# A two-block transformer on one core: ten planning rounds, weight chunks split ahead of the norms, and a shared scaling

## The chip, the cores and the metric

The kernel runs on one core of one Trainium2 chip. The metric is the device time of one execution in microseconds; of several runs the median is taken. Engines are called as in the profile: PE is TensorE (PEld its weight loads), DVE is VectorE, ACT is ScalarE, POOL is GpSimd, and SP is SyncE, whose queue issues most transfers (SPq).

## What is computed

One sequence of 512 tokens with 1024 channels passes two blocks, all in float32. The first block has two layers; each is a mixing part and a feed-forward part (FFN):

```python
h = rms_norm(x, norm_mix[l]) * (1.0 + sc1) + sh1
proj = h @ w_in[l]                      # delta-rule heads, windowed attention, gates
...
x = x + gt1 * (merged @ w_o[l])
h = rms_norm(x, norm_ffn[l]) * (1.0 + sc2) + sh2
up_act, up_lin = jnp.split(h @ w_up[l], 2, axis=-1)
up_act = causal_dwconv(up_act, ffn_conv[l]) + ffn_conv_b[l]
x = x + gt2 * ((jax.nn.silu(up_act) * up_lin) @ w_down[l])
```

The mixing part runs a gated delta rule over 8 heads in chunks and a sliding-window attention with sinks. The second block is one layer of the same make: norm, `w_in_2`, a banded attention, a state-space branch, gates, `w_out_2`, final norm. Scales and shifts (sc, sh, gt) come from `w_ada`.

## The kernel before

**Arithmetic.** A float32 product is made of three passes at a faster matmul type: weights and activations are split into a high part (`whi`, `hhi`) and a rest (`wlo`, `hlo`), and hi x hi, hi x lo and lo x hi are added up in PSUM. `chunk` (line 546) loads a weight chunk of 128x1024 elements into a `raw` tile from SP's queue, and `split` (line 539) makes `whi` by a copy on ACT and `wlo` by a subtraction on VectorE. `raw`, `whi` and `wlo` have three buffers each.

**GEMMs.** `gemm_f` (line 564) gives feature-major output, 256 columns of weights at a time: eight row tiles in two chunks of four, two PSUM tiles `gf`. With `split` it does the first 256 tokens of all chunks, then the other 256. `gemm_t` (line 600) gives token-major output in four PSUM tiles `gt`, one for each 128 tokens; the last `last` chunks are held, and each token tile is finished and passed on in turn.

**Seams.** `residual` (line 1421) calls `add` (line 1396): two `gemm_t` over the two halves of 512 output columns, with gate and addition into the x tiles on VectorE and the sum of squares on ACT. In the second half `done` calls `norm` (line 752) for the tile before: add and power on VectorE and POOL (`nsum`), scaling into `xn` on VectorE, four transposes `ntr` on TensorE for each half of the channels, scale and shift (VectorE for the first half, ACT for the second), `hhi` on ACT, `hlo` on VectorE. The next stage's matmuls need this h. There are four such seams: after mixing and after the FFN, in each layer. The next stage is `ffn` with `w_up`, then `delta_front` with columns 1024 on of `w_in`, and after the last FFN `second` with columns 2048 on of `w_in_2`; each begins with `gemm_f(..., split=True)`.

**Order.** Nothing is issued directly. A `Recorder` keeps all operations with their dependencies and a modelled duration (`cost`, line 112); `plan` (line 202) is a list scheduler that goes through time, takes on each engine the ready operation with the smallest priority `prio`, models buffers, transfers and ACT's function tables, and gives one order of all; `emit` (line 353) issues it. The priority is the place in the program, and tiles of one tag get their buffers in program order. All instructions come from line 359, so the profile's groups are told apart by tile names. `step` (line 633), called by every `chunk`, moves background work (the products with `w_ada`, tables of the state space) forward.

**The first norm** is another routine (`first_norm`, line 759); it leaves chunks of two row tiles in `self.pre`, from which `gemm_f` takes them in place of loading.

Of the kernel before, what the change touches and what calls it, by code (L numbers as in the profile page):

```python
# [50 lines left out]
LAT = {"PE": 54.0, "DVE": 35.0, "ACT": 60.0, "POOL": 110.0, "SP": 60.0}  # L51
SLACK = {"PE": 0.0, "DVE": 0.0, "ACT": 0.0, "POOL": 0.0, "SP": 0.0}
TABLES = {"Exp": ("exp",), "Tanh": ("exp", "silu", "gelu"), "Silu": ("silu",), "Sin": ("silu", "trig"), "Gelu_apprx_tanh": ("gelu",)}
# [3 lines left out]
class Op:  # L57
    __slots__ = ("n", "eng", "name", "call", "dur", "over", "lock", "dep", "succ", "left", "ready", "tiles", "need", "prio", "start", "mode", "bytes", "team", "lead", "wait", "tables")

# [19 lines left out]
class Recorder:  # L79
# [121 lines left out]

    def plan(self):
        import heapq
        ops = self.ops
        for o in ops:
            o.left = len(o.dep)
            o.ready = 0.0
            for p in o.dep.values():
                p.succ.append(o)

        uses, order, bufs, place = {}, {}, {}, {}
        for o in ops:
            o.need = []
            for t in o.tiles:
                nm = t.name
                if nm not in uses:
                    uses[nm] = 0
                    tag = t.tag
                    order.setdefault(tag, []).append(nm)
                    bufs[tag] = t.bufs or t.tag_meta.bufs  # L220
                    place[nm] = tag, len(order[tag]) - 1
                uses[nm] += 1
                o.need.append(place[nm])

        pend = None
        for o in ops:
            o.lead, o.team = o, [o]
            if o.eng != PE_E:
                continue
            key = o.tiles[-1].name, o.mode  # L230
            if pend and pend[1] == key and all(p.n < pend[0].n or p.eng == PE_E for p in o.dep.values()):
                o.lead = pend[0]
                o.lead.team.append(o)
            else:
                pend = (o, key) if o.mode != (128, 128) else None
        for o in ops:
            o.left -= sum(p.lead is o.lead for p in o.dep.values())
            o.lead.wait = len(o.lead.team)
        freed = {g: [0.0] * b for g, b in bufs.items()}
        turn = {g: 0 for g in bufs}  # L240
# [8 lines left out]
        mode, table = (128, 128), "exp"  # L249
        count = 0  # L250

        def offer(o):

            while o.need:
# [8 lines left out]
                since[tag, k] = t = heapq.heappop(freed[tag])  # L263
                turn[tag] += 1
                o.ready = max(o.ready, t)
                o.need.pop()
# [19 lines left out]
        seq = []  # L286
        import collections
        while count < len(ops):
# [11 lines left out]
            if best is None:  # L300
                raise RuntimeError("no plan: slots %s" % {g: (turn[g], len(order[g]), sorted(parked.get(g, {}))[:3]) for g in turn if parked.get(g)})
            s, e = best
# [4 lines left out]
            if e in held:  # L307
                other = held[POOL_E if e == DVE_E else DVE_E]
                if other > s + 140 and ops[av[0][1]].lock:
                    free = [x for x in av if not ops[x[1]].lock]  # L310
                    if free:
                        x = min(free)
                        av.remove(x)
                        heapq.heapify(av)
                        heapq.heappush(av, (-1, x[1]))
            p, n = heapq.heappop(av)
            for o in ops[n].team:
                o.start = s = max(s, clock[e])
                d = o.dur
                if e == PE_E and o.mode != mode:  # L320
# [5 lines left out]
                if o.lock:  # L326
                    s = max(s, held[POOL_E if e == DVE_E else DVE_E] - 140)
                    held[e] = s + d
                end = s + d
                clock[e] = end - o.over  # L330
                if o.name == "dma_start":
                    dma_free = max(dma_free, end) + o.bytes / 340.0
                    end = max(dma_free, end) + (2300 if e == SP_E else 2600)
                count += 1
                seq.append(o)
                for t in o.tiles:
# [3 lines left out]
                    if not uses[nm]:  # L340
                        heapq.heappush(freed[t.tag], last_end[nm])
                        wake(t.tag)
                for q in o.succ:
                    if q.lead is o.lead:
                        continue
                    q.left -= 1
                    q.ready = max(q.ready, clock[e] if q.eng == e == PE_E else end + LAT[q.eng] + (0 if q.eng == e else SLACK[q.eng]))
                    if not q.left:
                        offer(q)
        self.end = max(clock.values())  # L350
        return seq

# [18 lines left out]
class Net:  # L371
# [166 lines left out]

    def split(self, raw, n, eng=None):
        hi = self.p_hi.tile([128, 1024], F32R, name="whi", tag="whi")  # L540
        lo = self.p_lo.tile([128, 1024], F32R, name="wlo", tag="wlo")
# [4 lines left out]
    def chunk(self, parts, kk, n, eng=None):  # L546

# [7 lines left out]
        hi, lo = self.split(raw, kk * n, eng)  # L555
        self.step()
        return self.views(hi, lo, kk, n)

    @staticmethod
# [4 lines left out]
    def gemm_f(self, w, c0, act, consume, ntile=2, parts=None, split=False):  # L564
# [3 lines left out]
        for g in range(ntile // 2):  # L568
            ps = [self.Gp("gf") for _ in range(2)]
            c = c0 + g * 256  # L570
            cols = [(c, 256)] if parts is None else [(p, 128) for p in parts]
            m = 2 if (w.tensor.name, c, 0) in self.pre else 4
            groups = [(k0, min(m, kt - k0)) for k0 in range(0, kt, m)]

            def load(k0, n):
                if (w.tensor.name, c, k0) in self.pre:
                    return self.pre.pop((w.tensor.name, c, k0))
                return self.chunk([w[k0 * 128:(k0 + n) * 128, p:p + m] for p, m in cols], n, 256)
# [173 lines left out]
    def norm(self, xt, t, ss, a, b, h):  # L752
        rs = self.norm_scale(ss)
        for q in range(2):
            xn = self.t2("xn")
            self.tsc(xn, xt[:, q * 512:q * 512 + 512], rs, MUL)
            self.norm_half(xn, t, q, a, b, h)

    def first_norm(self, x0):
# [47 lines left out]
        for q in range(4):  # L807
# [10 lines left out]
            for c in (1024, 0):  # L818
                self.pre[w.tensor.name, c, 2 * q] = self.chunk([w[q * 256:q * 256 + 256, c:c + 256]], 2, 256, self.G)
            apply(q, row)  # L820
# [485 lines left out]
    def mixing(self, l, xin, xout, hact):  # L1306
# [88 lines left out]

    def add(self, w, act, xs, g=None, done=None):

        ss = [self.ts("nss", 2) for _ in range(4)]
        for c in range(2):
            o = slice(c * 512, c * 512 + 512)  # L1400

            def f(t, ps):
# [7 lines left out]
                if done:  # L1410
# [10 lines left out]
    def residual(self, w, act, xs, xout, g, a, b):  # L1421

# [5 lines left out]

        self.add(w, act, xs, g, done)
        return h  # L1430

    def ffn(self, l, hact, xin, xout):
# [551 lines left out]
```

## Time and profile before

| | us |
|---|---|
| median of three runs | 2430.78 |
| lowest and highest | 2430.03, 2432.83 |
| the profiled execution | 2433.17 |
| its span, first to last instruction | 2431.4 |

| engine | busy us | instructions |
|---|---|---|
| TensorE | 2364.1 | 13388 |
| VectorE | 1644.6 | 3087 |
| ACT | 1012.2 | 2095 |
| POOL | 522.9 | 719 |

Busy time counts the union of an engine's instructions. Matmuls overlap one another, so a busy TensorE may still be slowed; the granted clock (PEclk, a share of 2.4 GHz) tells one such slowing. In a timeline row the bracket gives the idle time of the engine ahead of the instruction and what ended it.

### The profile page before, as it was taken

What the parts mean: (1) busy time and instruction counts of PE and PEld (TensorE: products, weight loads), DVE (VectorE), ACT (ScalarE), POOL (GpSimd) and SP (SyncE); (2) the same over time, 40 slices, a digit from 0 to 9 for tenths busy, and PEclk for the clock granted to TensorE, in tenths of its full rate; (3) what the DMA queues carried; (4) which work ended last, traced back from release to release, by engine and by line L of the source; (5) the groups of instructions that cost most, each with busy time, mean ns of one, the idle gap of its engine ahead of it and who ended that gap; (6) DMA issues with size and microseconds to landing.
All of it is one profiled execution on the core that took longest, in us unless ns stands there. A gap on an engine that the chain in (4) does not pass through costs nothing.

```text
span 2431.4 us, 35819 instructions
## 1 busy us (share of the span) xinstructions
PE 2364.1 (97%) x13388; PEld 1928.4 (79%) x13388; DVE 1644.6 (68%) x3087; ACT 1012.2 (42%) x2095; POOL 522.9 (22%) x719
## 2 busy tenths in 40 slices
PE   7999999999999999999999999999999998999998
PEld 4878777778888887887888787888888888877786
DVE  3898899676666577468888955566555546765454
ACT  5544454533443233354446454334323323264432
POOL 1322424204100000213232421050051613500000
PEclk9999999999999999999999999999999999999999
DMA  7322225456446556332222333445334344532242
GB/s 251 99 66 77 84 71 161 139 168 200 156 153 197 180 181 187 118 103 74 66 75 79 89 111 96 130 170 184 114 109 127 117 146 146 173 113 79 78 139 78
DMA packets 239742, 309.10 MB, mean 127 GB/s; under 512 B 32144, under 2 KB 189712, under 8 KB 239568
## 3 DMA queue, kind: packets, MB, share of 16 engines
q1 hardware_dynamic: 228864, 275.64, 37.0%
q0 software_dynamic: 10416, 30.91, 3.5%
q8 instruction: 106, 1.74, 0.3%
q14 instruction: 68, 0.56, 0.1%
q10 hardware_dynamic: 288, 0.26, 0.0%
HBM read 276.20 MB, written 30.56 MB: 126 GB/s over the span
## 4 chain that ended last, share of the span: by engine, by line
PE 84%; DVE 7%; DMA 3%; ACT 2%; issue 2%; SPq 1%; POOL 1%; DVEq 0%; POOLq 0%; ACTq 0%
PE gf L359 54%; PE gt L359 18%; PE sc L359 1%; SPq L359 1%; PE pvo L359 1%; PE ada L359 1%; DMA pn<-nd 1%; PE zps L359 1%; PE osps L359 1%; PE kqs L359 1%; PE yps L359 1%; DVE wlo L359 1%; PE qktr L359 1%; PE gram L359 1%; DVE ua L359 1%
## 5 line engine op out<-in xcount | busy, mean ns | idle before, releaser
L359 PE MATMUL gf<-hhi,whi 128*128 128x512 f32 (+1 forms) x1888 | 720.8, 384 | 11.8 <-ACT whi L359 8.5
L359 PE MATMUL gf<-hlo,whi 128*128 128x512 f32 (+1 forms) x1888 | 720.6, 382 | 0.2 <-DVE hlo L359 0.2
L359 PE MATMUL gf<-hhi,wlo 128*128 128x512 f32 (+1 forms) x1888 | 719.9, 382 | 0.1
L359 DVE TENSOR_TENSOR wlo<-raw,whi 128x1024 fp32r<-128x1024 f32 (+1 forms) x358 | 461.8, 1291 | 339.2 <-ACT whi L359 336.1
L359 ACT ACTIVATE whi<-raw 128x1024 fp32r<-128x1024 f32 (+1 forms) x366 | 378.6, 1036 | 655.7 <-PE gf L359 310.5
L359 PEld LDWEIGHTS gf<-hhi,whi 128*128 128x128 f32 x1888 | 358.3, 191 | 76.2 <-ACT whi L359 10.0
L359 PEld LDWEIGHTS gf<-hlo,whi 128*128 128x128 f32 x1888 | 359.1, 190 | 60.7 <-issue 2.1
L359 PEld LDWEIGHTS gf<-hhi,wlo 128*128 128x128 f32 x1888 | 359.0, 190 | 59.4 <-DVE wlo L359 0.6
L359 PE MATMUL gt<-whi,g 128*128 128x512 f32 x704 | 220.1, 392 | 0.0
L359 PEld LDWEIGHTS gt<-whi,g 128*128 128x128 f32 x704 | 132.2, 188 | 27.2
L359 PE MATMUL gt<-wlo,g 128*128 128x512 f32 x352 | 137.4, 390 | 0.0
L359 DVE SCALAR_TENSOR_TENSOR acc<-raw,csil,acc 128x1024 f32<-128x1024 f32 x70 | 90.7, 1295 | 34.8 <-DMA raw<-in_w_ada_dram 34.6
L359 DVE SCALAR_TENSOR_TENSOR cacc<-gf,vec,cacc 128x511 f32<-128x511 f32 x144 | 106.8, 743 | 7.9 <-ACT cacc L359 6.6
L359 PE MATMUL gt<-whi,hhi 128*128 128x512 f32 (+1 forms) x288 | 107.1, 374 | 1.0 <-DVE gx L359 1.0
L359 PE MATMUL gt<-wlo,hhi 128*128 128x512 f32 (+1 forms) x288 | 107.6, 374 | 0.0
L359 PE MATMUL gt<-whi,hlo 128*128 128x512 f32 (+1 forms) x288 | 107.5, 375 | 0.0
L359 PE MATMUL gf<-rhi,whi 128*128 128x512 f32 x256 | 99.9, 390 | 0.0
L359 PE MATMUL gf<-rhi,wlo 128*128 128x512 f32 x256 | 99.8, 390 | 0.0
L359 PE MATMUL gf<-rlo,whi 128*128 128x512 f32 x256 | 99.8, 390 | 0.0
L359 DVE SCALAR_TENSOR_TENSOR facc<-gf,vec,facc 128x511 f32<-128x511 f32 x88 | 65.7, 748 | 37.2 <-ACT facc L359 35.6
L359 PEld LDWEIGHTS gt<-wlo,g 128*128 128x128 f32 x352 | 66.2, 188 | 13.5 <-issue 0.2
L359 POOL DMA_DIRECT2D acc<-in_b_ada_dram x4 | 2.1, 525 | 288.3 <-DVE wlo L359 283.5
(414 smaller groups left out, 3802.4 us busy)
## 6 DMA issues: line engine op xcount, KB each, us to landing
raw<-in_w_in_dram SPq DMA_DIRECT2D x140, 512.0 KB, 3.7
raw<-in_w_ada_dram SPq DMA_DIRECT2D x80, 512.0 KB, 4.0
raw<-in_w_up_dram SPq DMA_DIRECT2D x80, 512.0 KB, 4.2
raw<-in_w_down_dram SPq DMA_DIRECT2D x40, 512.0 KB, 3.7
wa<-in_w_ada_dram SPq DMA_DIRECT2D x32, 256.0 KB, 6.0
raw<-in_w_dn_out_dram SPq DMA_DIRECT2D x16, 512.0 KB, 3.5
raw<-in_w_swa_out_dram SPq DMA_DIRECT2D x16, 512.0 KB, 4.8
raw<-in_w_o_dram SPq DMA_DIRECT2D x16, 512.0 KB, 3.8
```

What stands on the lines that cost most here:

```text
L359: i = f(*a, **k).ins
```

## The change

Three things, in one diff.

- The planner runs up to ten rounds (`ROUNDS`). Each operation off TensorE is taken 30 ns longer (`MARGIN`), and a hand-over from one engine to another 30 ns longer (`SLACK`). After a round, `late` goes backward through the order and gives each operation a latest start, from its successors, the next operation on its engine and the next user of its buffers; the new priority is the mean of the old one (in the first round the start) and this. Buffers of a tag are then handed out in the order of the last plan. The plan with the earliest modelled end is issued; a round that finds no plan ends the loop.
- `ahead` loads and splits the first 256 columns of the next stage's weights (two chunks of four row tiles) just before the second `gemm_t` of `residual`, into tiles of their own: one buffer of each b4 lane and one of tag `ua`. `gemm_f` finds them in `self.pre` (the key now holds the offset of the layer, too).
- In `norm` the scaled tile `xn` of the second half is made by ACT (`Copy` with a scale), no longer by VectorE.

```diff
+MARGIN, SLACK = 30.0, 30.0
+ROUNDS = 10
...
             for o in ops[n].team:
-                o.start = s = max(s, clock[e])
-                d = o.dur
+                s = max(s, clock[e])
+                d = o.dur + (0 if e == PE_E else MARGIN)
...
+    def late(self, seq):
+
+        late, after = {}, {}
+        for o in reversed(seq):
+            took, x = o.end - o.start, self.end
+            f = after.get(o.eng)
+            if f is not None:
+                x = late[f.n] - min(f.start - o.start, o.dur - o.over)
+            for q in o.succ:
+                if q.eng != o.eng or q.eng != PE_E:
+                    x = min(x, late[q.n] - took - LAT[q.eng])
+            for t in o.tiles:
+                if t.name in self.then:
+                    x = min(x, late[self.first[self.then[t.name]]] - took - 60)
+            late[o.n] = x
+            after[o.eng] = o
+        return late
+
+    def plan(self):
+
+        self.prepare()
+        tags, best = self.tags, None
+        for k in range(ROUNDS):
+            seq = self.schedule(tags)
+            if seq is None:
+                break
+            if best is None or self.end < best[0]:
+                best = self.end, seq
+            self.first, tags = {}, {}
+            for o in seq:
+                for t in o.tiles:
+                    if t.name not in self.first:
+                        self.first[t.name] = o.n
+                        tags.setdefault(t.tag, []).append(t.name)
+            late = self.late(seq)
+            for o in self.ops:
+                o.prio = 0.5 * ((o.prio if k else o.start) + late[o.n])
+        self.end, seq = best
         return seq
...
+    def ahead(self, w, c):
+
+        pair = self.p_qk.tile([128, 2, 1024], F32R, name="wah", tag="ua", bufs=2)
+        homes = ((self.b4("wah", (128, 1024), F32R, "f"), self.b4("wah", (128, 1024), F32R, "x")), (pair[:, 0], pair[:, 1]))
+        for i, home in enumerate(homes):
+            self.pre[w.tensor.name, w.offset + c, 4 * i] = self.chunk([w[i * 512:i * 512 + 512, c:c + 256]], 4, 256, home=home)
...
             xn = self.t2("xn")
-            self.tsc(xn, xt[:, q * 512:q * 512 + 512], rs, MUL)
+            if q:
+                self.act(xn, xt[:, 512:1024], AF.Copy, scale=rs)
+            else:
+                self.tsc(xn, xt[:, 0:512], rs, MUL)
...
-        return self.residual(io["w_o"][l], mh, self.load_x(xin, "x"), xout, g, *self.mods(l, 1))
+        return self.residual(io["w_o"][l], mh, self.load_x(xin, "x"), xout, g, *self.mods(l, 1), (io["w_up"][l], 0))
...
+            if c and nxt:
+                self.ahead(*nxt)
             self.gemm_t([w[:, o]], act, f, last=2 + c)
...
-        h = self.residual(wd[c:FF], g, xs, xout, gr, a, b)
+        nxt = (io["w_in"][l + 1], 1024) if l + 1 < DEPTH else (io["w_in_2"][0], 2048)
+        h = self.residual(wd[c:FF], g, xs, xout, gr, a, b, nxt)
```

## Rows read from the trace of the kernel before

**Rows 1.** The page's first part: busy us, share of span, instructions.
```profile
span 2431.4 us, 35819 instructions
PE 2364.1 (97%) x13388; PEld 1928.4 (79%) x13388; DVE 1644.6 (68%) x3087; ACT 1012.2 (42%) x2095; POOL 522.9 (22%) x719
```

**Rows 2.** Window view: length, busy us by engine, PEclk, DMA share, GB/s.
```profile
0.00:48.00 48.00, 35.03 (x181) 19.16 (x182) 12.05 (x35) 28.17 (x50) 9.42 (x16) 1.00 0.91 292
48.00:640.00 592.00, 580.22 (x3709) 467.75 (x3708) 474.48 (x1053) 269.49 (x686) 174.03 (x209) 1.00 0.39 118
640.00:660.00 20.00, 15.61 (x83) 13.53 (x82) 17.28 (x35) 12.68 (x27) 3.62 (x5) 0.83 0.70 241
652.00:658.00 6.00, 4.84 (x22) 4.55 (x23) 5.39 (x10) 2.20 (x6) 0.27 (x1) 0.50 0.81 250
...
1015.00:1050.00 35.00, 28.91 (x162) 24.90 (x161) 22.81 (x48) 17.39 (x37) 6.34 (x8) 0.90 0.36 115
1050.00:1638.00 588.00, 583.24 (x3782) 473.41 (x3781) 435.38 (x990) 265.11 (x675) 161.89 (x192) 1.00 0.33 98
1638.00:1660.00 22.00, 17.64 (x116) 16.33 (x116) 15.27 (x31) 11.75 (x26) 3.17 (x4) 0.84 0.63 216
1660.00:2003.00 343.00, 343.00 (x1619) 285.01 (x1618) 188.82 (x217) 119.86 (x156) 93.74 (x205) 1.00 0.41 129
2003.00:2038.00 35.00, 29.05 (x154) 25.45 (x153) 22.21 (x48) 14.91 (x36) 7.33 (x8) 0.85 0.37 126
2038.00:2290.00 252.00, 246.75 (x1360) 199.88 (x1360) 162.10 (x272) 111.35 (x196) 47.89 (x44) 1.00 0.38 119
```

**Rows 3.** Timeline of the first seam: start us, duration us, instruction, idle before.
```profile
646.65 0.39 PE L359 MATMUL gt<-whi,mlo 128*128 128x512 f32 x1
...
650.63 2.35 DVE L359 TENSOR_TENSOR wlo<-raw,whi 128x1024 fp32r<-128x1024 f32 x2
...
651.87 0.55 PE L359 MATMUL gf<-hhi,whi 128*128 128x256 f32 x1 [3.23 <-ACT whi L359]
...
658.85 1.29 DVE L359 TENSOR_TENSOR hlo<-xn,hhi 128x512 fp32r<-128x512 f32 x2 [1.45 <-ACT hhi L359]
```

**Rows 4.** Timeline of the fourth seam, TensorE's two waits.
```profile
2020.51 1.09 PE L359 MATMUL gf<-hhi,whi 128*128 128x256 f32 x4 [2.24 <-ACT hhi L359]
...
2028.54 1.94 PE L359 MATMUL ntr<-cst,xn 128*128 128x128 f32 x8 [3.07 <-DVE xn L359]
```

**Rows 5.** Groups by form: count, busy us, mean ns, idle before.
```profile
L359 DVE TENSOR_TENSOR wlo<-raw,whi 128x1024 fp32r<-128x1024 f32 x344 | 450.8, 1312 | 314.8 <-ACT whi L359 311.9 <-PE bt L359 1.6
...
L359 DVE TENSOR_SCALAR xn<-x,nsum 128x512 f32<-128x512 f32 x32 | 14.7, 482 | 5.3 <-POOL nsum L359 5.3
...
L359 ACT ACTIVATE whi<-raw 128x1024 fp32r<-128x1024 f32 x344 | 363.8, 1059 | 619.1 <-PE gf L359 309.1 <-PE gt L359 184.0 <-issue 53.8
...
L359 ACT ACTIVATE cacc<-gf,vec 128x512 f32<-128x512 f32 x48 | 32.9, 685 | 22.5 <-PE gf L359 20.2 <-DVE vt L359 1.5 <-POOL kd L359 0.3
```

**Rows 6.** Timeline, third seam: two neighbours of the 256-column matmuls.
```profile
1654.09 0.28 PE L359 MATMUL gf<-hhi,whi 128*128 128x256 f32 x1
1654.21 0.28 PE L359 MATMUL gf<-hlo,whi 128*128 128x256 f32 x1
```

**Rows 7.** Timeline of the first mixing stage: a wait and a long operation.
```profile
105.75 2.12 DVE L359 TENSOR_SCALAR pn<-pn 64x256 f32<-64x256 f32 x1 [2.88 <-DMA pn<-nd]
...
110.78 0.66 PE L359 MATMUL qktr<-cst,qk 128*128 128x128 f32 x4 [2.35 <-DVE xi L359]
```

More of the change, by code (lines that the diff above doesn't have):

```diff
@@ L57 @@
 class Op:
-    __slots__ = ("n", "eng", "name", "call", "dur", "over", "lock", "dep", "succ", "left", "ready", "tiles", "need", "prio", "start", "mode", "bytes", "team", "lead", "wait", "tables")
+    __slots__ = ("n", "eng", "name", "call", "dur", "over", "lock", "dep", "succ", "left", "ready", "tiles", "need", "prio", "start", "end", "mode", "bytes", "team", "lead", "wait", "tables")
 class Eng:
@@ L199, in add, with prepare @@
         return o
-    def plan(self):
-        import heapq
+    def prepare(self):
         ops = self.ops
         for o in ops:
-            o.left = len(o.dep)
-            o.ready = 0.0
             for p in o.dep.values():
                 p.succ.append(o)
-        uses, order, bufs, place = {}, {}, {}, {}
+        self.uses, self.bufs, self.tags = {}, {}, {}
         for o in ops:
-            o.need = []
             for t in o.tiles:
                 nm = t.name
[L216 to L223, printed above, removed]
+                if nm not in self.uses:
+                    self.uses[nm] = 0
+                    self.tags.setdefault(t.tag, []).append(nm)
+                    self.bufs[t.tag] = t.bufs or t.tag_meta.bufs
+                self.uses[nm] += 1
         pend = None
@@ L235, in plan, with schedule @@
                 pend = (o, key) if o.mode != (128, 128) else None
+    def schedule(self, tags):
+        import heapq
+        ops, bufs = self.ops, self.bufs
+        uses = dict(self.uses)
+        place = {nm: (g, k) for g, names in tags.items() for k, nm in enumerate(names)}
         for o in ops:
-            o.left -= sum(p.lead is o.lead for p in o.dep.values())
+            o.need = [place[t.name] for t in o.tiles]
+            o.ready = 0.0
+            o.left = len(o.dep) - sum(p.lead is o.lead for p in o.dep.values())
             o.lead.wait = len(o.lead.team)
-        freed = {g: [0.0] * b for g, b in bufs.items()}
+        freed = {g: [(0.0, "")] * n for g, n in bufs.items()}
         turn = {g: 0 for g in bufs}
@@ L250, in plan @@
         count = 0
+        self.then = {}
         def offer(o):
@@ L262, in offer @@
                     return
-                since[tag, k] = t = heapq.heappop(freed[tag])
+                since[tag, k], old = heapq.heappop(freed[tag])
+                self.then[old] = tags[tag][k]
                 turn[tag] += 1
-                o.ready = max(o.ready, t)
+                o.ready = max(o.ready, since[tag, k])
                 o.need.pop()
@@ L300, in plan @@
             if best is None:
-                raise RuntimeError("no plan: slots %s" % {g: (turn[g], len(order[g]), sorted(parked.get(g, {}))[:3]) for g in turn if parked.get(g)})
+                return None
             s, e = best
@@ L328, in plan @@
                     held[e] = s + d
+                o.start = s
                 end = s + d
@@ L333, in plan @@
                     end = max(dma_free, end) + (2300 if e == SP_E else 2600)
+                o.end = end
                 count += 1
@@ L346, in plan @@
                     q.left -= 1
-                    q.ready = max(q.ready, clock[e] if q.eng == e == PE_E else end + LAT[q.eng] + (0 if q.eng == e else SLACK[q.eng]))
+                    q.ready = max(q.ready, clock[e] if q.eng == e == PE_E else end + LAT[q.eng] + (0 if q.eng == e else SLACK))
                     if not q.left:
@@ L536, in rsqrt, with split @@
         return m
-    def split(self, raw, n, eng=None):
-        hi = self.p_hi.tile([128, 1024], F32R, name="whi", tag="whi")
-        lo = self.p_lo.tile([128, 1024], F32R, name="wlo", tag="wlo")
+    def split(self, raw, n, eng=None, home=None):
+        hi, lo = home or (self.p_hi.tile([128, 1024], F32R, name="whi", tag="whi"),
+                          self.p_lo.tile([128, 1024], F32R, name="wlo", tag="wlo"))
         self.act(hi[:, :n], raw[:, :n], AF.Copy)
@@ L554, in chunk @@
             o += c
-        hi, lo = self.split(raw, kk * n, eng)
+        hi, lo = self.split(raw, kk * n, eng, home)
         self.step()
         return self.views(hi, lo, kk, n)
+    def ahead(self, w, c):
[3 more added lines that the diff above has]
+            self.pre[w.tensor.name, w.offset + c, 4 * i] = self.chunk([w[i * 512:i * 512 + 512, c:c + 256]], 4, 256, home=home)
     @staticmethod
@@ L1419, in add, with residual @@
             done(3, ss[3])
-    def residual(self, w, act, xs, xout, g, a, b):
+    def residual(self, w, act, xs, xout, g, a, b, nxt):
         h = self.new_h()
@@ L1427, in done @@
             self.norm(xs[t], t, ss, a, b, h)
-        self.add(w, act, xs, g, done)
+        self.add(w, act, xs, g, done, nxt)
         return h
```

20 lines of the change are left out of this document (10 added, 10 removed).

## The prediction

> **What bounds the kernel now.** I read the page's busy table first: TensorE is busy 2364.1 of 2431.4 us [rows 1], so at most 67 us are idle, and the other engines matter only where TensorE waits for them. Next I cut the span into stages with the window view [rows 2]. In the pure matmul stage from 1660 to 2003 TensorE is busy 343.00 of 343.00 us, while VectorE has 188.82 and ACT 119.86: nothing there can be gained by ordering, and both helpers have room. The loss stands at the four seams, where a norm turns x into the next h and every further matmul needs that h: 640 to 660 (after mixing, layer 0), 1015 to 1050 (after the FFN, layer 0), 1638 to 1660 and 2003 to 2038 (the same in layer 1).
>
> A seam costs twice: idle time, and after it matmuls at a lower clock. From 652 to 658 the granted clock is 0.50, the 1.2 GHz level, right behind a 3.23 us wait [rows 2, 3]. So I price a seam as (window minus PE busy) plus (1 minus PEclk) times window. First: 4.39 + 0.17 x 20 = 7.8. Second: 6.09 + 0.10 x 35 = 9.6. Third: 4.36 + 0.16 x 22 = 7.9. Fourth: 5.95 + 0.15 x 35 = 11.2. Sum 36.5 us. Outside, the two mixing stages idle 11.8 and 4.8 us and the second block 5.3 [rows 2], together 21.9.
>
> What ends the waits: at the first seam TensorE has done a few matmuls of the next stage when it stops for whi, from ACT, until 651.87 [rows 3]. The weights had to be split in the seam itself, between norm operations, because all three whi buffers hold the last w_o chunks to the end; wlo is written at 650.63, in the middle of the norm. At the fourth seam it waits 2.24 us for hhi of an early tile, then 3.07 us at the transposes of the last tile, behind xn [rows 4].
>
> **Part 1, two chunks ahead.** ahead() loads and splits the first column group of the next GEMM (two chunks, 4 x 128 rows by 256 columns each) before the chunks of the second half of the residual GEMM, into homes of its own. It issues two loads on SP's queue, two ACT copies of 1.06 us and two VectorE subtractions of 1.31 us [rows 5]; they are only moved, no byte is added. In the plan's first order they stand ahead of the residual GEMM's own loads on SP: those wait behind them if a raw buffer is late. Cover: the matmul stages, with VectorE busy 55% and ACT 35% [rows 2]; without it a seam would pay 2 x (1.06 + 1.31) = 4.7 us, as now. On the seam the 3.23 us wait at 651.87 goes, and I take the third seam for its twin (idle 4.36 against 4.39 [rows 2]). What is late next is h of the last tile. Built from rows, its chain after the last residual matmul is two VectorE passes of some 0.69, ACT's square about 0.8, the sum and power about 0.8, the scale 0.7, transposes 0.6, four scalings 1.4, hhi 0.6 and hlo 0.7: about 7 us, with a dozen hand-overs about 8.5 (an estimate; the 0.65 us of one hlo is half the 1.29 of [rows 3], the other pieces are close to such passes). Measured today it is longer: at the first seam the last hlo begins at 658.85, 12 us after the last residual matmul at 646.65 [rows 3], since ACT and VectorE do four splits in between. Against it TensorE has the first token half of two column groups, 2 x 48 matmuls at 0.12 us [rows 6] = 11.5 us. The second of these groups still needs whi and wlo in the seam, but has 5.7 us for it and finds the three whi buffers free and its loads done. So I let nearly all go, but not the wait for the early tile, which no weight cures: I leave 1.5 us at each mixing seam and 3.0 at each FFN seam (the 2.24 plus a hand-over), 9.0 in all. Gain 36.5 - 9.0 = 27.5 us. Bounds: 12 if only the first group is covered (rival B), 36.5 if no loss is left.
>
> **Part 2, the shared scale.** For the second half of each row tile xn moves from VectorE to ACT: 16 instructions of 0.482 us [rows 5] leave VectorE, and ACT gets 16. The trace has no ACT copy of this shape with a per-row scale from SBUF; nearest is the 128x512 one with a scale at 0.685 us [rows 5]. One tile's two halves then take 0.69 side by side instead of 2 x 0.482 in a row: 0.3 us off a tile's chain. Behind it on ACT wait the scalings and hhi of the same tile; if it queues behind a 1.06 us split, the chain loses up to 0.8 instead. I take nothing (bounds from 1 us less to 3 us more over the four seams, since one tile a seam is exposed).
> The row says VectorE is the fuller engine in the seam, 17.28 of 20 us against ACT's 12.68 [rows 2]. The Trainium skill (Perfetto Trace Analysis, Optimizing Scalar/DVE Operations) says that an operation for which VectorE has a fast mode is quicker there, and that moving it to ACT pays if VectorE is saturated. By its first half the move loses 0.2 us each on ACT, by its second it gains; at 86% I read the row as near the second, and neither changes the sum.
>
> **Part 3, ten plans.** The order on every engine is fixed at build time by a list scheduler. Its priority was the place in the program; now it becomes, in nine further rounds, the mean of the old priority and a latest start computed backward from the end, buffers may be handed out in the order of the last plan, each non-TensorE operation gets 30 ns margin, and each hand-over between engines 30 ns. Kept is the plan that ends first by the planner's own clock. No instruction is added or removed. What can it win on the chip? Only the 21.9 us idle outside the seams, and waits where the planner was wrong: at 110.78 TensorE waits 2.35 us for a transpose's input, because VectorE was held by a 2.12 us operation on 64x256 [rows 7], far over the 0.482 of the 128x512 one [rows 5]. A margin of 30 ns doesn't cover such an operation, but small lateness it does. Bounds: all 21.9 gone, or the same again added. Nearest to the truth I think is a fifth gone: 4 us. At the head (idle 13 of 48 us, DMA share 0.91 [rows 2]) the transfers decide, so I take 0, within 3 either way.
>
> **The sum.** The profiled execution took 2433.2 us (span 2431.4 and 1.8 around it): 2433.2 - 27.5 - 4 = 2401.7. The median of the runs is 2430.8, 2.4 lower, so 2399.
>
> **Rivals.**
> A, the forecast: 2399. Chance 0.42.
> B, only the first group is covered. ACT and VectorE come to the second group's split too late, as they did at 650.63 [rows 3]; TensorE then has 5.7 us against a chain of about 10, idles 4 us per seam and pays some 2 more at the low clock: 24 of 36.5 us stay. 2430.8 - 12 - 4 = 2415. For it: VectorE's 86%; against: four splits become two. Chance 0.20.
> C, the new orders also clear two thirds of the idle time outside: 2430.8 - 27.5 - 15 = 2388. For it: with program order a chain step goes as soon as it is ready, so each lateness becomes a wait; with latest starts some stand further back. Chance 0.16.
> D, it does not do what it says: the homes of the early chunks come free only at the seam (they take the last buffer of three tags) and the new plans shift waits about. 2431, give or take 5. Against: x, its row and the activations leave one buffer each. Chance 0.10.
> E, slower. Rounds chosen by a clock that takes 0.29 us (152 + 0.53 x 256 ns, in cost) for an operation that took 2.12 put more matmuls behind late VectorE results in the mixing stages. A wait like that of rows 7 costs 2.35 us, and half of a low-clock stretch behind it; at the first seam that stretch was 2 x 0.17 x 20 = 6.8 us, and I take one half as long, so 1.7 us. At 4 us each, 8 new ones eat the 31.5 us gain; 12 give 2430.8 + 48 - 31.5 = 2447. Chance 0.12. The Trainium skill (TensorE: Matmul & The Clock Gate, Architectural detail) says that matmuls keep their order and that VectorE and ACT work strictly first in, first out, which is what makes one misplaced instruction hold all behind it; the 2.35 us row agrees.
>
> **How the numbers follow.** 0.2% (4.9 us) is about what measurements of this kernel can tell from no change. A, B and C lie below 2425.9, and a little of D: faster 0.79. Same 0.09, most of D. Slower 0.12, E. The range leaves out E and the far end of C: 2376 to 2432.
>
> **What would show it.** Right: no TensorE wait for whi at the seams, PEclk near 1.00 in windows of 20 to 35 us there, PE idle in them under 3 us each, the same matmul count, ACT with 16 more xn. Part 3 shows in idle time of the two mixing stages, 16.6 us now. Wrong: a half-clock stretch left at three or four seams (B, D), or mixing stages that are longer with new waits over 1 us (E).

## The result, and the profile after

The changed kernel takes 2453.31 us (2449.80 to 2455.23), the kernel before beside it 2430.41 us: ratio 1.0089, 95% interval 1.0074 to 1.0104. It is slower by 0.89%, some 22 us, where the forecast said faster by 32. The profiled execution took 2451.6 us, and this is its first part (us, share of the span, instructions):

```profile
span 2449.8 us, 35838 instructions
PE 2369.8 (97%) x13388; PEld 1947.0 (79%) x13388; DVE 1637.8 (67%) x3071; ACT 1020.1 (42%) x2111; POOL 517.7 (21%) x719
```

Against [rows 1] the work is the same: as many matmuls, sixteen instructions moved from VectorE to ACT. So the 18.4 us of the two spans are waiting and low clock. The window view of the changed kernel, with windows laid about the same work as in [rows 2] (length, busy us by engine, granted clock, DMA share, GB/s); the eighth is a part of the first:

```profile
48.00:652.00 604.00, 587.75 (x3702) 480.55 (x3701) 464.68 (x1052) 270.56 (x684) 168.01 (x197) 0.97 0.39 117
652.00:673.00 21.00, 16.86 (x95) 14.62 (x94) 16.62 (x34) 15.50 (x33) 4.94 (x5) 0.84 0.64 216
1027.00:1062.00 35.00, 29.11 (x181) 25.88 (x180) 20.82 (x43) 19.91 (x42) 6.66 (x9) 0.95 0.35 108
1062.00:1650.00 588.00, 578.11 (x3751) 475.54 (x3750) 438.86 (x985) 264.62 (x677) 163.79 (x190) 0.99 0.33 98
1650.00:1672.00 22.00, 17.66 (x109) 15.81 (x108) 15.72 (x32) 13.16 (x28) 4.37 (x4) 0.84 0.60 195
1672.00:2027.00 355.00, 347.14 (x1632) 288.25 (x1631) 194.71 (x218) 119.29 (x155) 89.07 (x204) 0.99 0.41 127
2027.00:2062.00 35.00, 30.30 (x172) 26.34 (x171) 20.70 (x44) 17.76 (x40) 4.82 (x12) 0.90 0.39 130
410.00:455.00 45.00, 35.16 (x332) 27.53 (x332) 25.06 (x60) 14.40 (x33) 7.39 (x16) 0.63 0.27 80
```

PEclk has two decimals, too coarse for 600 us, so I summed for each stage what a matmul takes to the next one's start beyond the median of its kind (its output tile) and shape; I call that the excess. It holds idle time and low clock together. The stages are the windows of [rows 2] and of the view above; the second block is 2062 to 2314 in the changed kernel.

| stage | excess before, us | after |
|---|---|---|
| first mixing stage | 38.8 | 52.8 |
| second mixing stage | 29.7 | 34.2 |
| the four seams | 7.8, 10.2, 7.1, 10.9 = 36.0 | 7.1, 8.4, 7.5, 8.5 = 31.5 |
| second FFN's matmul stage | 1.0 | 11.6 |
| second block | 12.6 | 10.4 |
| all of the program | 139.1 | 160.4 |

The seams, where 27.5 us were to come from, gave 4.5. Two places lost more than that, and the second mixing stage lost as much.

**The end of the first mixing stage.** From 410 to 455 us TensorE is busy 35.16 of 45 us at a clock of 0.63; in the kernel before the like stretch reads:

```profile
400.00:445.00 45.00, 41.84 (x241) 33.16 (x240) 33.79 (x98) 24.67 (x55) 18.26 (x33) 0.99 0.47 145
```

The timeline of the changed kernel there (start, duration, instruction, idle before):

```profile
444.58 2.07 PE L406 MATMUL kqs<-st,qk 128*128 128x128 f32 x8 [0.44 <-DVE st L406]
...
451.42 2.07 PE L406 MATMUL kqs<-st,qk 128*128 128x128 f32 x8 [0.44 <-DVE st L406]
453.10 1.09 ACT L406 ACTIVATE mb<-gf 128x512 f32<-128x512 f32 x2 [1.88 <-PE kqs L406]
...
453.75 0.79 PE L406 MATMUL gf<-hhi,whi 128*128 128x512 f32 x1 [0.26 <-ACT mb L406]
```

These are the steps of the delta recurrence, one behind the other, and no gf matmul of the gates between them. Each lasts 6.8 us, with TensorE at the 1.2 GHz level:

```profile
430.00:453.00 23.00, 19.22 (x91) 16.70 (x92) 5.32 (x17) 5.78 (x14) 0.58 (x1) 0.50 0.09 28
```

The next gate GEMM comes only when ACT empties its PSUM tile into mb, and ACT's wait before that is put down by the profile to the recurrence's last kqs.

**The second FFN.** TensorE waits 7.86 us for one wlo (same view):

```profile
1844.24 0.69 DVE L406 TENSOR_TENSOR xm<-gt,grow 128x512 f32<-128x512 f32 x1 [1.10 <-PE gt L406]
1844.97 9.15 DVE L406 TENSOR_TENSOR x<-x,xm 128x512 f32<-128x512 f32 x1
1845.05 0.31 POOL L406 TENSOR_TENSOR sbb<-sbb,stmp 128x64 f32<-128x64 f32 x1
...
1856.38 0.79 PE L406 MATMUL gf<-hhi,wlo 128*128 128x512 f32 x1 [7.86 <-DVE wlo L406]
```

The addition x + xm, mostly 0.69 us, takes 9.15, beside a run of 30 POOL operations of the state-space tables. VectorE's next wlo is late by that much.

**The first seam.** The whi wait of [rows 3] is gone, as forecast, and others stand there:

```profile
663.38 2.67 POOL L406 TENSOR_TENSOR nsum<-nsum,mhalf 128x1 f32<-128x1 f32 x1 [0.57 <-DVE nsum L406]
664.48 0.80 PE L406 MATMUL gf<-hhi,wlo 128*128 128x256 f32 x2 [2.27 <-DVE wlo L406]
...
666.86 1.97 PE L406 MATMUL ntr<-cst,xn 128*128 128x128 f32 x8 [1.58 <-ACT xn L406]
```

### The profile page after: what moved, and what is told of

The parts are those of the page before. It is cut to its first block, busy times and chain, and to the rows that moved or that the text cites. A ratio compares the mean times of both kernels' runs of the same rounds, so it can differ in the third digit from the quotient of the medians.

```text
span 2449.8 us, 35838 instructions
## 1 busy us (share of the span) xinstructions
PE 2369.8 (97%) x13388; PEld 1947.0 (79%) x13388; DVE 1637.8 (67%) x3071; ACT 1020.1 (42%) x2111; POOL 517.7 (21%) x719
## 4 chain that ended last, share of the span: by engine, by line
PE 90%; DVE 3%; ACT 2%; DMA 2%; issue 2%; SPq 0%; POOL 0%; DVEq 0%; POOLq 0%; ACTq 0%
PE gf L406 57%; PE gt L406 19%; PE sc L406 1%; PE osps L406 1%; PE gram L406 1%; PE pvo L406 1%; PE kqs L406 1%; PE zps L406 1%; PE yps L406 1%; PE xps L406 1%; PE ada L406 1%; PE ntr L406 1%; PE bs L406 1%; DMA wa<-in_w_ada_dram 1%; PE qktr L406 1%
## 5 line engine op out<-in xcount | busy, mean ns | idle before, releaser
L406 PE MATMUL gf<-hhi,wlo 128*128 128x512 f32 (+1 forms) x1760 | 682.3, 389 | 13.8 <-DVE wlo L406 13.8
L406 PE MATMUL gf<-hlo,whi 128*128 128x512 f32 (+1 forms) x1760 | 682.9, 389 | 0.3 <-DVE hlo L406 0.3
L406 PE MATMUL gf<-hhi,whi 128*128 128x512 f32 (+1 forms) x1760 | 682.1, 390 | 1.1 <-ACT mb L406 0.7
L406 DVE TENSOR_TENSOR wlo<-raw,whi 128x1024 fp32r<-128x1024 f32 (+2 forms) x350 | 444.6, 1270 | 318.9 <-ACT whi L406 317.8
L406 ACT ACTIVATE whi<-raw 128x1024 fp32r<-128x1024 f32 (+2 forms) x358 | 370.6, 1037 | 625.8 <-PE gf L406 360.7
L406 PEld LDWEIGHTS gf<-hhi,wlo 128*128 128x128 f32 x1760 | 333.2, 189 | 75.2 <-DVE wlo L406 15.3
L406 PEld LDWEIGHTS gf<-hlo,whi 128*128 128x128 f32 x1760 | 332.7, 189 | 64.0 <-issue 3.6
L406 PEld LDWEIGHTS gf<-hhi,whi 128*128 128x128 f32 x1760 | 333.0, 190 | 62.8 <-ACT hhi L406 2.3
L406 DVE SCALAR_TENSOR_TENSOR cacc<-gf,vec,cacc 128x511 f32<-128x511 f32 (+1 forms) x144 | 106.1, 742 | 18.1 <-ACT cacc L406 17.0
L406 DVE SCALAR_TENSOR_TENSOR acc<-raw,csil,acc 128x1024 f32<-128x1024 f32 x70 | 91.8, 1311 | 31.6 <-DMA raw<-in_w_ada_dram 31.0
L406 ACT ACTIVATE pp<-sc,snm 128x128 f32<-128x128 f32 x128 | 45.5, 365 | 46.5 <-DVE snm L406 36.5
```

The source lines that it names most:

```text
L406: i = f(*a, **k).ins
```

## The experiments

All times are medians; the ratio is to the kernel before on the same chip. "One round" is ROUNDS = 1, that is, priority by place in the program as in the kernel before; "no margins" is MARGIN = SLACK = 0.

| label | kernel | us | ratio, 95% interval |
|---|---|---|---|
| r1 | changed kernel, one round | 2484.4 | 1.0217, 1.0202 to 1.0232 |
| r1_m0 | changed kernel, one round, no margins | 2439.6 | 1.0035, 1.0023 to 1.0047 |
| plan_only | changed kernel without early chunks and shared scale | 2456.7 | 1.0099, 1.0084 to 1.0114 |
| ahead_only | before + early chunks | 2444.4 | 1.0047, 1.0030 to 1.0064 |
| m0 | changed kernel, no margins | 2438.8 | 1.0024, 1.0014 to 1.0034 |
| scale_only | before + shared scale | 2427.8 | 0.9979, 0.9970 to 0.9988 |
| rounds_scale | before + shared scale + ten rounds | 2428.2 | 0.9991, 0.9981 to 1.0001 |
| ahead_half | before + first early chunk only | 2436.1 | 1.0019, 1.0005 to 1.0033 |
| r1_margin | as r1, operation margin alone | 2478.7 | 1.0197, 1.0175 to 1.0220 |
| r1_slack | as r1, hand-over margin alone | 2447.8 | 1.0070, 1.0050 to 1.0091 |
| ahead_dve | ahead_only, table products on VectorE | 2431.5 | 1.0001, 0.9991 to 1.0010 |
| r1_m0_dve | r1_m0, table products on VectorE | 2426.7 | 0.9981, 0.9972 to 0.9990 |
| ad_lag4000 | r1_m0_dve, last transposes planned 4 us later | 2426.1 | 0.9974, 0.9963 to 0.9986 |
| ad_lag2000 | the same, 2 us | 2425.8 | 0.9972, 0.9962 to 0.9982 |
| sd_lag4000 | ad_lag4000 without early chunks | 2430.3 | 0.9996, 0.9987 to 1.0006 |
| ad_ex | r1_m0_dve, dependences of h by pieces | 2401.6 | 0.9868, 0.9853 to 0.9883 |
| sd_ex | ad_ex without early chunks | 2407.1 | 0.9895, 0.9879 to 0.9912 |
| before_ex | before, dependences of h by pieces | 2413.9 | 0.9920, 0.9905 to 0.9934 |

### Which part costs it

Three theories: P, the backward priorities cost the time; W, the early chunks and the shared scale do; M, the 30 ns margins do.

```diff
-ROUNDS = 10
+ROUNDS = 1
```

> The changed kernel with one planning round: program order is the priority again, margins, early chunks and shared scaling stay. Theory P (the backward priorities cost what the change lost): well under the changed kernel's 2453, at 2415 to 2430 us, and no stretch near 410 to 455 us in which TensorE runs chain steps alone. Theory W (early chunks or the shared scaling cost it): 2445 to 2455 us. Theory M (the 30 ns margins spoil the order): 2440 to 2455 us.

```diff
-MARGIN, SLACK = 30.0, 30.0
-ROUNDS = 10
+MARGIN, SLACK = 0.0, 0.0
+ROUNDS = 1
```

> As the kernel with one round, and both margins at zero: the kernel before plus early chunks and shared scaling, nothing else. P: 2405 to 2425 us, the seams' part of the forecast alone (27.5 us at best). W: 2440 to 2455. M: under the one-round kernel with margins by over 10 us.

Without early chunks and shared scale, with the ten rounds and the margins:

```diff
-            if c and nxt:
-                self.ahead(*nxt)
...
-            if q:
-                self.act(xn, xt[:, 512:1024], AF.Copy, scale=rs)
-            else:
-                self.tsc(xn, xt[:, 0:512], rs, MUL)
+            self.tsc(xn, xt[:, q * 512:q * 512 + 512], rs, MUL)
```

> The kernel before plus the ten planning rounds with margins; no early chunks, no shared scaling. P: 2450 to 2465 us, slower than before by at least what the whole change is, as the early chunks no longer help. W: 2420 to 2430 us. M: 2445 to 2460.

The early chunks alone (one round, no margins, and the last five lines of that diff):

> The kernel before plus the two early chunks alone, one round, no margins. P with my forecast of the seams: 2403 to 2420 us, and no wait for whi at the first and third seam. If the seam is bound by the norm's chain and not by the split: 2420 to 2430 us. W: 2440 us or more.

P falls: with the margins in place, the nine further rounds gain 31 us (2484.4 to 2453.3). The margins cost 45 in one round (2439.6 to 2484.4); r1 came out above the ranges of all three theories. W holds for the early chunks: alone they add 11 to 13 us. The parts don't add: plan_only costs 1.0% and r1_m0 0.35%, but together 0.9%. Each order puts the POOL runs (see below) beside other work: a wlo takes 11.38 us at 1834.85 in plan_only, and two take 9.82 in r1_m0, at 597.33 and 1592.37; how much of the difference that makes is not shown.

### What the rounds are worth, and the scale

Three kernels without margins: `m0` is the changed kernel with this line alone changed; `scale_only` has also one round and no early chunks (the first two lines of the diff above left out); `rounds_scale` is that with ten rounds.

```diff
-MARGIN, SLACK = 30.0, 30.0
+MARGIN, SLACK = 0.0, 0.0
```

> The changed kernel with its ten rounds, early chunks and shared scale, but without the 30 ns margin and the 30 ns per hand-over. With one round the same kernel took 2439.6 us. Theory M2 (the rounds only win back what the margins spoil; by the planner's own clock they win 26 us with margins, 2424.3 to 2398.0, and 5 without, 2365.1 to 2360.2): 2435, and the idle stretch of chain steps alone at the end of the delta part of the first mixing stage is gone, excess of TensorE there near 45 us as with one round. Theory M1 (the rounds win the same 31 us as they did with margins, 2484.4 to 2453.3): 2409.

> The kernel before with the shared scale alone. If the parts add up: 2431.2 minus what it gave beside the early chunks (2444.4 to 2439.6, 4.8 us) = 2426, with waits at the last tile's transposes of under 2 us at the fourth seam. If it helped only because the early chunks load VectorE: 2431.

> The kernel before with shared scale and ten rounds, no margins, no early chunks (the planner's own clock: 2364.3 in the first round, 2358.8 in the second). Theory M2: 2426 minus about 5 = 2421. Theory M1: 2426 minus 31 = 2395. Slower than the kernel with the shared scale alone would say that the later rounds' order is worse on the chip than by the planner's clock.

M2 holds in the main, though it had m0 and rounds_scale 4 and 7 us lower: without margins ten rounds and one can't be told apart (1.0024 and 1.0035 with early chunks, 0.9991 and 0.9979 without). What the rounds gain in the changed kernel is some of what its own margins had lost. That isn't the same as doing nothing: by the excess the rounds take 13 us from the first mixing stage in m0 (45.1 in r1_m0, 32.2 in m0) and 9 in rounds_scale, and in the profiled executions they lose as much and more elsewhere, in m0 most of it in the second FFN (2.8 to 12.4), where a POOL run holds an x + xm for 11.22 us at 1824.25. The shared scale alone gives 0.21%, about 5 us.

### Which margin

```diff
-MARGIN, SLACK = 30.0, 30.0
-ROUNDS = 10
+MARGIN, SLACK = 30.0, 0.0
+ROUNDS = 1
```

> The changed kernel with one round and the 30 ns margin of each operation outside TensorE alone (no 30 ns per hand-over). With both it took 2484.4 us, with neither 2439.6. Theory Mo (the per-operation margin does it: VectorE and POOL, nearly full in the mixing stages, look overfull to the planner, the delta chain falls behind in the plan, and the filler matmuls are used up before it ends): 2475, the 8 us waits of the delta chain's end near 450 and 1470 are still there. Theory Ms (the hand-over slack does it, since a chain is a row of hand-overs): 2445, no such waits.

The other way round, MARGIN = 0 and SLACK = 30:

> The changed kernel with one round and the 30 ns per hand-over between engines alone. Theory Mo: 2445, no 8 us waits near 450 and 1470. Theory Ms: 2475, with them.

Mo: the operation margin costs 39 us (1.0197 against 1.0035), the hand-over margin 8.5. Most of it lies in the mixing stages (excess some 112 us in the two together against some 79 without margins). Timeline of the kernel with the operation margin:

```profile
440.87 0.71 PE L406 MATMUL osps<-xs,ua 128*128 128x128 f32 x4 [1.27 <-ACT xs L406]
...
450.03 1.97 PE L406 MATMUL otr<-cst,ot 128*128 128x128 f32 x8 [8.45 <-POOL ot L406]
```

The recurrence's end, here the norm of its output ot, stands bare, as the recurrence does at 410 to 455 in the changed kernel, where the rounds repair it in part. How the margin does it is argued and not shown: 1053 VectorE instructions of the stage [rows 2] with 30 ns each are 31.6 us on top of 474 busy ones in 592, so the planner may count VectorE 85% busy instead of 80% and use up the matmuls that would cover the recurrence before it ends. The theory's words on VectorE and POOL, "nearly full", go beyond the rows: 80% and 29% [rows 2].

### The early chunks and the POOL runs

The pair of the second early chunk takes one of the two buffers of the tag `ua`, which the state-space tables (`sws`) use too. `ahead_half` drops that pair:

```diff
-        pair = self.p_qk.tile([128, 2, 1024], F32R, name="wah", tag="ua", bufs=2)
-        homes = ((self.b4("wah", (128, 1024), F32R, "f"), self.b4("wah", (128, 1024), F32R, "x")), (pair[:, 0], pair[:, 1]))
+        homes = ((self.b4("wah", (128, 1024), F32R, "f"), self.b4("wah", (128, 1024), F32R, "x")),)
```

> The kernel before with the first of the two early chunks alone (the pair of buffers that it shares with the state-space tables is not taken; the second chunk is split in the seam). With both it took 2444.4 us. Theory U (the second chunk takes a buffer of the tables, which moves a burst of POOL table operations into the w_o GEMMs, where a VectorE subtraction then takes 9 to 10 us): the 3.3 us waits at 605 and 1603 and the half-clock stretch behind them go, no wlo over 6 us there, 2432 or less. Theory Q (early loads and splits cost by themselves, in the queues): half of the 13 us stay, 2438, with the long wlo still there.

The waits at 605 and 1603 go, as U wants, but the time falls only to 2436: a POOL run now meets a wlo at 1821.24 (8.78 us for one of 0.69), and TensorE waits 6.59 us there. The eight executions lie between 2431.5 and 2443.7 us, and the trace is that of the 2443.7; whether the run meets the wlo in the shorter ones is not shown. So the pair decides where a run falls, not whether one can do harm. The next two take POOL out of it, by this edit in all six operations of the product:

```diff
             def cm(o, a, b, tmp=tmp):
-                self.tt(o[0], a[0], b[0], MUL, self.G)
+                self.tt(o[0], a[0], b[0], MUL)
...
```

> The kernel before with the early chunks, and the 6-operation complex products of the state-space tables (10 products for each of four groups) on VectorE instead of POOL. With them on POOL it took 2444.4 us. Theory V (a run of POOL operations locks a VectorE operation out until it ends): no wlo over 4 us, the 3.4 us TensorE waits at 605 and 1603 and the slow matmuls behind them gone, 2434 or less. Rival: the long subtraction comes from something else, or VectorE's added work costs as much: 2444 or more.

> The kernel before with early chunks, shared scale, and those products on VectorE (one round, no margins). With them on POOL 2439.6 us; the shared scale without early chunks 2427.8. Theory V: 2429. If the early chunks are worth something at the seams once the bursts are out of the way, it comes out below 2427.8 by what the seams show; if they only cost, above it, with nothing to be seen at 605 and 1603.

Timeline with the early chunks and products on POOL:

```profile
598.59 9.82 DVE L406 TENSOR_TENSOR wlo<-raw,whi 128x1024 fp32r<-128x1024 f32 x1 [3.20 <-ACT whi L406]
...
607.02 0.31 POOL L406 TENSOR_TENSOR sws<-sws,stmp 128x64 f32<-128x64 f32 x1
607.40 1.16 POOL L406 TENSOR_TENSOR stmp<-pw,sbc 128x64 f32<-128x64 f32 x1
...
609.07 0.50 PE L406 MATMUL gt<-whi,mhi 128*128 128x512 f32 x1 [3.27 <-DVE mb L406]
```

and with the products on VectorE:

```profile
597.89 1.23 DVE L406 TENSOR_TENSOR wlo<-raw,whi 128x1024 fp32r<-128x1024 f32 x1 [3.20 <-ACT whi L406]
```

V holds: the same subtraction takes 1.23 us instead of 9.82, the wait is gone, and the time is 11 to 13 us lower in both pairs (1.0047 to 1.0001, 1.0035 to 0.9981), although VectorE has 240 instructions more. The planner does allow for VectorE and POOL holding each other up (`held` in its code), but only to the end of one operation, not of a run.

With the runs away the early chunks seem worth nothing: 0.9981 with them, 0.9979 for the scale alone (scale_only, where no run makes TensorE wait). But that pair differs in the products' engine too. The pair below that differs in the early chunks alone, ad_lag4000 and sd_lag4000, gives them some 4 us (0.9974 and 0.9996).

### Why the seams keep their loss

First the order: the transposes of each norm's last tile are taken as ready later, in the planner alone (lag is 4000 or 2000 ns for these transposes and 0 for all else).

```diff
...
-                    q.ready = max(q.ready, clock[e] if q.eng == e == PE_E else end + LAT[q.eng] + (0 if q.eng == e else SLACK))
+                    q.ready = max(q.ready, clock[e] if q.eng == e == PE_E else end + LAT[q.eng] + (0 if q.eng == e else SLACK + q.lag))
...
```

> The kernel with early chunks, shared scale and table products on VectorE (2426.7 us), and in the planner alone the transposes of each norm's last tile are taken as ready 4.0 us later (4 x 2 x 4 instructions; nothing is added or removed). There the four seams wait for these transposes 3.93, 1.92 + 2.65, 3.93 and 5.76 us, with some 16 first-half matmuls of 96 done before them at the first seam. Theory O (the order: the cover that the forecast counted on stands behind a waiting transpose in TensorE's queue): these waits shrink to under 1.5 us each and the half-clock stretch behind them shortens, 2408 to 2416. Theory L (the chain itself is longer than all that could cover it): the waits turn up at hhi or hlo of the same tile, 2422 or more.

> As the first, with 2.0 us instead of 4.0. Theory O: half of it, waits at the last tile's transposes about 2 us shorter at each seam, 2414 to 2421. Theory L: 2424 or more.

> The same 4.0 us for the last tile's transposes, with shared scale and table products on VectorE, without the early chunks. Theory O with early chunks of worth: the first two column groups are split in the seam, TensorE waits there for whi or wlo as the kernel before does (3.4 us), so 6 us or more above the kernel with them. If early chunks aren't what covers the chain: within 3 us of it.

Neither dose moved a wait: 3.77, 1.76 + 2.49, 3.77 and 5.59 us stand as they stood, within 0.04. Theory O as put falls. Without the early chunks the time is 4.3 us higher, between the two bounds set down; in sd_lag4000 the lag did move a wait, from the last transposes (3.29 us in scale_only) to wlo (4.84), so part of the 4.3 may be the lag's. Theory L looked right, but its waits at hhi or hlo didn't turn up either, and no matmul had moved ahead of the transposes. This shows why; the window view of the kernel r1_m0_dve for gf matmuls alone (us and count; PE first), from the last residual matmul to the last transposes, and the row of those:

```profile
646.30:652.70 6.40, 1.95 (x12) 1.54 (x12) 0.00 (x0) 0.00 (x0) 0.92 0.66 208
```

```profile
652.72 1.97 PE L406 MATMUL ntr<-cst,xn 128*128 128x128 f32 x8 [3.77 <-DVE hlo L406]
```

Twelve, not 96. Six per column group: those of feature block 0 (two column tiles, three passes). The planner took an access to SBUF as one interval from its first to its last element. A norm writes 128 tokens in four blocks of 512, so the write of the last tile seems to touch the first tokens of blocks 1 to 3, and a matmul on them is planned behind it. The edit, for hhi and hlo alone, in parts (step, many and w are distance, number and width of the pieces, and meet() compares them piece by piece):

```diff
             hi = f0 + sum(s * (c - 1) for s, c in dims[1:]) + 1
...
-            return name, t, (p0, p0 + dims[0][1], f0, hi)
+            return name, t, (p0, p0 + dims[0][1], f0, hi, step, many, w)
...
-                    hit = a0 < r[1] and r[0] < a1 and b0 < r[3] and r[2] < b1
+                    hit = a0 < r[1] and r[0] < a1 and b0 < r[3] and r[2] < b1 and meet(e[2], r)
```

> Early chunks, shared scale, table products on VectorE (2426.7 us), and one edit in the planner's test of dependences: for hhi and hlo an access of four feature blocks by 128 tokens counts as its four pieces, no longer as one interval from its first to its last element. As one interval the last tiles' writes seem to touch the first tokens of blocks 1 to 3, and indeed only the 12 matmuls of block 0 run in the first seam before the last tile's transposes (646.37 to 648.67), 84 of the 96 that the forecast counted as cover run behind them; a later ready time for these transposes moved none. Theory R (this false dependence is why the early chunks cover nothing): some 90 first-half matmuls stand ahead of the last transposes, the seam waits of 3.93, 1.92 + 2.65, 3.93 and 5.76 us fall under 1.5 each, 2398 to 2410. Theory L (chain longer than the cover in any order): 2418 or more.

> The same without the early chunks. If the early chunks are worth what the forecast took from them once the cover is there: TensorE waits in each seam for whi or wlo as before, 10 us or more above the kernel with them. If the cover alone is what counts, and the splits fit beside it: within 4 us of it.

> The kernel before with the edit of the dependence test alone. Theory R: the four seams lose about what they lose in the kernel without early chunks, and the shared scale's 4 us come on top: 2404 to 2416. Theory L: 2425 or more.

The same two views for ad_ex:

```profile
648.10:654.50 6.40, 5.77 (x49) 5.59 (x47) 0.00 (x0) 0.00 (x0) 1.00 0.61 192
```

```profile
654.56 0.60 PE L414 MATMUL ntr<-cst,xn 128*128 128x128 f32 x4
655.12 0.60 PE L414 MATMUL ntr<-cst,xn 128*128 128x128 f32 x4
```

and its four seams as windows:

```profile
640.00:662.00 22.00, 22.00 (x159) 20.47 (x158) 17.46 (x36) 15.69 (x33) 4.06 (x6) 1.00 0.70 237
1010.00:1045.00 35.00, 34.39 (x240) 31.38 (x239) 23.80 (x48) 21.34 (x44) 5.44 (x8) 1.00 0.34 108
1618.00:1640.00 22.00, 22.00 (x155) 20.29 (x154) 18.35 (x38) 16.71 (x36) 4.30 (x6) 1.00 0.73 240
1980.00:2015.00 35.00, 34.47 (x229) 31.03 (x229) 20.76 (x44) 17.91 (x41) 5.44 (x8) 1.00 0.39 132
```

R holds. TensorE is busy through both mixing seams and at full clock in all four; the seams' excess is 0.2, 1.6, 0.2 and 1.2 us, 3.2 in all against 31.2 in r1_m0_dve, and the time falls by 1.13% (0.9981 to 0.9868), 27 us. The expectation was off in one point: 49 matmuls stand ahead of the last transposes, not some 90; the first group's first half is enough. Without early chunks the seams' excess is 8.4 us and the time 5.5 us higher, neither the 10 nor the "within 4" that were set down. The dependence alone, in the kernel before, is worth 0.80%, 20 us; there the 3.23 us wait for whi still stands in both mixing seams. ad_ex beats both kernels, by 1.3% and, from the two ratios, 2.2%.

## Why the prediction was wrong, step by step

- **What bounds the kernel**: right for the seams. They held 36 us by the excess, 36.5 by [rows 2], and ad_ex has taken 33 of them. But 29 us of excess came in outside them, in the two mixing stages and the second FFN, where the forecast had 4 us less.
- **Part 1, the cover, is the step that failed.** The forecast set a chain of 8.5 us against 2 x 48 first-half matmuls, since the weights were split and the matmuls' operands written. That was read from the code's data flow, not from the trace: in the kernel before, too, only 10 of the narrow matmuls run before the last transposes at 654.64, and the few of them around the wait of [rows 3] could have been counted. What the planner believes of a dependence decides what is cover. The runs show in its place that at each seam of the changed kernel 84 of the 96 stood behind the last transposes, and the seams gave 4.5 us. With the dependence by pieces the forecast's gain of 27.5 comes in full, but most of it from the edit that the change doesn't make; the early chunks bring 5.5.
- **Part 1, the chain**: 8.5 us was too short. In ad_ex it takes 11.1, from the last residual matmul at 647.60 to the end of the last hlo at 658.75; in the kernel before it took 13.5 (646.65 to 658.85 and 1.29 more, [rows 3]). Early chunks, shared scale and the rest together gave 2.4 us of the 5 assumed.
- **Part 1, the cost**: taken as nothing, covered by a VectorE busy 55%. It was 11 to 13 us, none of it from VectorE's share: the new pair shifts the tables' buffers and with them a POOL run. The forecast named the homes' tags (rival D) but not who else rotates through them.
- **Part 2**: taken as 0 between 1 less and 3 more; it gave 5 us alone (2.9 to 7.3 by its interval), beyond the bound or at it. In scale_only the wait for whi at the mixing seams is gone without any early chunk; 0.57 us for wlo and 3.29 us at the last transposes stand in its place. ACT's copy takes 0.724 us, near the 0.69 assumed from [rows 5]. With the cover there the seams without early chunks fall from 18.5 us (before_ex) to 8.4 (sd_ex), where the scale and the products on VectorE came together; their shares were not separated.
- **Part 3**: taken as 4 us gained, it is some 14 lost (2439.6 without rounds and margins, 2453.3 with both). Its bounds, all 21.9 us gone or the same again added, held it; the value inside did not. The forecast saw the margin as weak protection against lateness. It is a wrong duration, for thousands of short operations; that the plan's order follows it is the reading argued above, not shown.
- **The rivals**: E, slower by late results in the mixing stages, gave 2447 against 2453 and the right stage. Its mechanism is not shown: the cost came from the margins and a POOL run, not from misjudged long operations, so the nearness of its number is luck. Its reading of [rows 7] was short, too: the 2.12 us operation ends at 107.87, and in the 2.35 us that TensorE then waits VectorE does a wlo and steps for xt and qk. B's sign of a half-clock stretch left at the seams was there, for another reason.

Open: the changed kernel's own order was run neither with the products on VectorE, which would say how much of its second-FFN wait goes, nor with the dependence by pieces. How a margin moves the recurrence in the plan is open too.

## What to carry to other kernels

Before matmuls are counted as cover for a chain, count in the trace how many of them run before the chain's next step today; if few do although their operands are ready, look for what the order's maker believes, first of all strided writes taken as one interval. A safety margin per operation is not neutral in a list schedule: 30 ns cost 39 us here, probably since it stretches most the engine with the most short instructions. And an edit that takes a buffer of a shared tag moves everyone else in that tag, so ask what that work locks.

## What was not expected of the hardware

A VectorE operation with two SBUF operands beside a run of short POOL operations can lose far more than one of them: 1.23 us became 9.82 beside 24 POOL operations, 0.69 became 9.15 beside 30. The POOL operations of such a run overlap by some 0.03 us. In the rows of ahead_only above the subtraction gets through at the first break, 0.07 us before 607.40, and the POOL product beside it takes 1.16 us where those before it take 0.28. Over the traces of all kernels here 36 VectorE operations of two tensors (TENSOR_TENSOR) took over 2.5 us beside eight or more POOL operations. None of them was held past a break; 26 got through at the first, and ten before any. What lets the ten through is not shown, nor why the same x + xm took only 1.57 us at 1841.57 in the changed kernel and got through three POOL operations later, in an unbroken run. An operation of 0.69 us with one operand in PSUM, xm <- gt, grow at 1844.24, kept its length within such a run. The other way round a POOL power of 0.56 us took 2.67 in the seam at 663.38 while VectorE worked on wlo and two hlo without a pause.

The Trainium skill (SBUF — State Buffer, Who interferes with whom) says that VectorE and GpSimd share one pair of ports as an exclusive lock, that a VectorE instruction with two SBUF inputs contends with a GpSimd instruction that reads SBUF, and that one with at most one SBUF input, outside the two-port modes, doesn't. The rows agree with both. Of the two-port modes it says that whoever issues first has the pair for the whole instruction and that the other side blocks fully; here, with two SBUF inputs, one operation was blocked through 24 and through 30 instructions, and by these rows an unbroken run is what counts.
